# The prologue and the first mixer of a two-layer trunk written as one planned task list, with two DMA queues

## The chip, the cores and the metric

The program runs on one core of a Trainium2 chip as one launch. The metric is the device time of that launch in microseconds. The kernel before takes 1396.52 us, the median of 3 runs (1395.69 to 1398.09).

## The reference

The trunk has 512 tokens of width 1024 and two layers, all in float32. Layer 0 mixes tokens by windowed attention and by a depthwise convolution of 31 taps side by side, layer 1 by a scanned state space, and a gated feed-forward net follows each. Every norm is scaled, shifted and gated by vectors that are products of `silu(c)` with `w_mod`. Cut to the part around the change:

```python
silu_c = jax.nn.silu(c)
mod = (silu_c @ w_mod[i] + b_mod[i])[:, None, :]
sh_m, sc_m, g_m, sh_f, sc_f, g_f = jnp.split(mod, 6, axis=-1)
h = rmsnorm(x, norm_mix[i]) * (1.0 + sc_m) + sh_m
...
proj = h @ w_in + b_in
q, k, v, conf_in = jnp.split(proj, [ATTN_WIDTH, ATTN_WIDTH + KV_WIDTH,
                                    ATTN_WIDTH + 2 * KV_WIDTH], axis=-1)
attn = swa_sink_attention(q, k, v, sinks, positions)
conf = conformer_conv(conf_in, conv_w, conv_b, ln_g, ln_b)
return jnp.concatenate([attn, conf], axis=-1) @ w_out
...
a, g = jnp.split(u, 2, axis=-1)
h = causal_dwconv(a * jax.nn.sigmoid(g), conv_w, conv_b)
```

## The kernel before, in words

Activations lie with their 1024 features in 8 tiles of 128 partitions, and 512 tokens in the free dimension. A float32 product is made of three matmuls: each factor is cut into a head (`wh`, `hn` with h; ACT writes it, L299) and a rest (`wl`; DVE writes it, L304), and `mm3` (L351 to L353) adds head times head, head times rest and rest times head. Weights come as a stream of 128x1024 tiles (`raw`, 512 KB, L291) into 3 buffers; so a load waits for the rest of an earlier tile, and a product for the head and the rest of its own.

The stages are a prologue, mixer 0, a boundary in halves of 256 columns, the feed-forward net, and the same again for layer 1. Only the prologue and mixer 0 concern us.

**Prologue** (L620 to L760). It squares x for the norm, and for each of 8 steps (`kt`) it loads two 512 KB pieces of `w_mod` (`wss`) and one 384 KB piece of the input projection (`wg`). Two `mod_dot`s on DVE (L569) give the scale and the shift of the step, L695 and L700 write the normed tile's product and rest, ACT its head, and `begin` (L704) issues 18 matmuls into six PSUM banks `g0`, which hold the value and gate halves of convolution channels 0 to 2. The last step's 18 go through `mm3`. The rest of each `wg` tile is made on POOL (`split(g0r[kt], wh, wl, nc.gpsimd)`, L278). POOL also makes the rotary angles: some 35 small instructions (L1132 to L1188), then eight that spread them (L1205); ACT takes their sines (L747), and PE and ACT turn them into tables. Everything here is in the order in which it is written, with loads three steps ahead.

**Mixer 0.** Its work is a list of tasks with an engine, a cost and predecessors each. `Plan.run` (L129) simulates them with these costs and emits each engine's instructions in the order in which the simulation starts them; the table `MIXER0` adds a weight to each label and group. The tasks are: eight products of weight tiles (the value and gate of convolution channel 3, k, v, four q); for each of four channel groups a sigmoid, a product on DVE (`gated`), a store of the result to DRAM (`conv_store`, L792), four loads that read it back shifted (`conv_fetch`, L804, tile `s`, 270 KB each), a load of the taps as block-diagonal matrices (`conv_taps`, L797, 512 KB each) and 64 matmuls (`conv_product`, L811); four attention heads of scores, maxima, exponentials (L921), turns (L941), values, reciprocals spread over rows (L973); the norm of the convolution; and the output products. Beside that, 24 pieces of `w_mod` are loaded (L561) and dotted (L569); the boundary needs the first eight.

The shifted loads read overlapping windows, four taps by 32 channels by 540 tokens:

```python
nc.sync.dma_start(u4[g], bass.AP(src.tensor, src.offset + 32 * g * CROW,
                                 [[1, CTAPS], [CROW, 32], [1, CWIN]]))
```

All these DMAs are issued by SP. SP, like every engine, runs in order: a DMA that has to wait for a buffer holds what is behind it. The n-th DMA of SP also waits for the (n-8)-th to land, since eight semaphores count them.

Of the kernel before, what the change touches and what calls it, by code (L numbers as in the profile page):

```python
# [39 lines left out]
_VEC = [("bmod", 96), ("nmix", 16), ("nffn", 16), ("fnorm", 8), ("bin", 14), ("ccw", 124),  # L40
# [30 lines left out]
EARLY = 2  # L71
# [6 lines left out]
MIXER0 = {'sigmoid': -134, 'square': 32, 'osq_add': 34, 'head': -75, 'tap0': -113, 'attn_h': 106, 'conv_h': 47, 'out_c': 124, 'gated': 56, 'rest': 35, 'values': 23, 'rope': -136, 'rstd': 138, 'mod_sum': 7, 'attn_l': 28, 'var': -26, 'turn': 5, 'mod_end': 106, 'exp': -35, 'bring': -32, 'conv_sum': 54, 'out_a': -99, 'osq': -119, 'mod_act': -104, 'mod_add': 39, 'mod_free': 120, 'normalize': -150, 'load': -55, 'product': 71, 'mean_row': -71, 'mod_dve': 105, 'tap': -30, 'recip': 55, 'ln': 121, 'centre': 30, 'residual': -18, 'maxima': 26, 'rstd_row': 20, 'conv_l': 108, 'mean': 47, 'rope_in': 141, 'v_bias': 101, 'mod_load': 69, 'mod_dot': -97, 'root': -10, 'rows': -58, 'rows_in': 61, 'v_turn': 7, 'v_in': -3, 'mod 2': 18, 'head 0': 104, 'mu': -68, 'keys': 27, 'conv 0': 16, 'head 1': -47, 'mod 1': -115, 'head 3': -150, 'shifts': -127, 'scores': 66, 'mod 0': 94, 'conv 3': -77, 'conv 2': 93, 'cbias': -51, 'conv': -113, 'store': -126, 'taps': -47, 'conv 1': 18, 'head 2': 150}  # L78
# [14 lines left out]
class Task:  # L93
    def __init__(self, ways, after, take, give, bonus):
        self.ways, self.after, self.take, self.give, self.bonus = ways, after, take, give, bonus
        self.next = []
# [10 lines left out]
class Plan:  # L107
# [4 lines left out]
    ENGINES = ("PE", "ACT", "DVE", "POOL", "DMA", "SIDE")  # L112

# [4 lines left out]
    def add(self, label, eng, cost, fn, after=(), take=None, give=None, bonus=0.0, table=None):  # L118
        return self.either(label, [Way(eng, cost, fn, table=table)], after, take, give, bonus)

    def either(self, label, ways, after=(), take=None, give=None, bonus=0.0):
        t = Task(ways, [a for a in after if a is not None], take or {}, give or {}, bonus)
        t.label, t.group = label, self.group
        for a in t.after:
            a.next.append(t)
        self.tasks.append(t)
        return t

    def run(self, weight, dry=False):  # L129
        room = dict(self.room)  # L130
        height, wait, at = {}, {}, {}
        for n, t in reversed(list(enumerate(self.tasks))):
            height[t] = min(w.cost for w in t.ways) + max([height[n] + self.LATENCY for n in t.next], default=0.0)
            wait[t], at[t] = len(t.after), 0.0
# [7 lines left out]
        for t in self.tasks:  # L142
            if not t.after:
                release(t)
        free = dict.fromkeys(self.ENGINES, 0.0)
        free.update(self.busy)
        left, now, ends = len(self.tasks), 0.0, []
        gone, table = set(), None
        while left:
            again = True  # L150
            while again:
                again = False
                for e in self.ENGINES:
# [23 lines left out]
                    free[e] = now + w.cost + cold  # L177
                    if w.table not in (None, table):
                        free[e] += self.TABLE
                        table = w.table  # L180
# [29 lines left out]
def trunk(ctx: ExitStack, tc: tile.TileContext, xT_d, vecs_d, rows_d, dsk_d, pos_d, const_d, wss_d, wg0_d,  # L210
          w_d, wmod_d, wdt_d, wcv_d, out_d):
# [68 lines left out]
    class Stream:  # L280
# [47 lines left out]
        def plan(self, plan, count, bonus, more, pool=True):  # L328


            out, last, prev = [], None, None
            for i in range(self.taken, self.taken + count + more):
                n = _STREAM[i] / 8
                t = None
                if i >= len(self.hl):
                    if i >= len(self.raw):
                        last = t = plan.add("load", "DMA", 1.46 * n, lambda i=i: self.load(i + 1), [last], dict(raw=1))
# [206 lines left out]
    def condition(cp):  # L544

        cb = cp.tile([P, KT * P], F32, name="cb")
        mod_pool.append(cb)
        c_ = con[:, 2 * P:]
        act(c_, c_, AF.Silu)
        for i in range(2):  # L550
            ps = spread(c_[:, 4 * i:4 * i + 4])
            yield
            nc.vector.tensor_copy(cb[:, i * T:(i + 1) * T], ps)
            yield

# [3 lines left out]
    def mod_load(n):  # L559
        t_ = mod_raw()  # L560
        nc.sync.dma_start(t_, wmod_d[n])  # L561
        return t_
# [35 lines left out]
    def plan_mods(plan, lo, hi, early):  # L598

        ends, dots, loaded = [], [], None  # L600
        for n in range(lo, hi):
            st, plan.group = {}, f"mod {n // 8}"

            def load(st=st, n=n):
                st["r"] = mod_load(n)

            if n < len(early):
                st["r"] = early[n]
            else:
                loaded = plan.add("mod_load", "DMA", 1.46, load, [loaded], dict(mr=1))  # L610
            dots.append(plan.add("mod_dot", "DVE", 1.22, lambda st=st, n=n: mod_dot(st["r"], mod_at(n)),
                                 [loaded], None, dict(mr=1)))
            if n % 8 == 7:
                ends.append(plan.add("mod_end", "DVE", 0.15, lambda n=n: mod_end(MOD_ORDER[n // 8]), dots))
                dots = []
# [6 lines left out]
    def even_layer(lp, cp, dp0):  # L622
# [5 lines left out]
        def load_first(j):  # L628
            ssr.append([])
            for i in range(2):  # L630
                t_ = mod_raw()
                nc.sync.dma_start(t_, wss_d[j, i])
                ssr[j].append(t_)
            t_ = wp.tile([P, NG0, P], F32, tag="raw", name=nm("raw"), bufs=3)
            nc.sync.dma_start(t_, wg0_d[j])
            g0r.append(t_)

# [3 lines left out]
        for kt in range(KT):  # L641
            nc.sync.dma_start(x[:, kt, :], xT_d[:, kt, :])
        nc.sync.dma_start(vecs, vecs_d)
        ssr, g0r, hn = [], [], []
        for j in range(3):
            load_first(j)
        cond = condition(cp)
        step(cond)

        acc = new_ssq()  # L650
        act(acc, x[:, 0, :], AF.Square)
        late = None
        for k in range(1, KT):
            sq = tmp()
            act(sq, x[:, k, :], AF.Square)
            if k < KT - 1:
                tt(acc, acc, sq, ALU.add)
            else:
                late = sq
            if k in (3, 4):  # L660
                step(cond, 2)
        for i, wch in enumerate((1, 4, 7, 10)):
            ts(b1[:, i, :], bm[:, wch, :], 1.0, None, ALU.add)
        gain = small(8)
        tt(gain, b1[:, 0, :], vec("nmix", 0, 8), ALU.mult)
        act(small(1), eps[:, 0:1], AF.Sqrt)
        g0 = [bank() for _ in range(NG0)]

# [5 lines left out]
        warm(WARM[0])  # L674
        total = token_sums([late, acc])
        warm(WARM[1])
        angles = []
        angle = rope_angles(lp, tile_s, angles)
        rope_t = {}
        tables = rope_tables(angles, tile_s, rope_t)  # L680
        step(angle, 14)

        def scale(kt):
            G = modv[:, 1, kt:kt + 1]
            mod_dot(ssr[kt][0], G)
            act(G, G, AF.Identity, bias=gain[:, kt:kt + 1], scale=vec("nmix", kt))

        def shift(kt):
            S = modv[:, 0, kt:kt + 1]
            mod_dot(ssr[kt][1], S)  # L690
            act(S, S, AF.Identity, bias=bm[:, 0, kt:kt + 1])

        def scaled(kt):
            t = tmp()
            stt(t, x[:, kt, :], modv[:, 1, kt:kt + 1], rb, ALU.mult, ALU.mult)  # L695
            return t

        def lower(kt, t):
            h, l = hn[kt]
            stt(l, t, modv[:, 0, kt:kt + 1], h.bitcast(F32), ALU.add, ALU.subtract)  # L700

        def begin(kt, w, a):
            for i in range(NG0):
                mm(g0[i], lhsT=w[:, i, :], rhs=a, start=(kt == 0 and w is wh and a is hn[0][0]), stop=False)  # L704

        wh = t = early = None
        for kt in range(KT):
            scale(kt)
            if kt == 0:
                col0 = rstd_cols(total, 1024.0)  # L710
                rb = spread(col0)
                warm(WARM[2])
                shift(kt)
            else:
                lower(kt - 1, t)
            t = scaled(kt)
            if kt > 0:
                begin(kt - 1, wh, hn[kt - 1][1])
            wh = wp.tile([P, NG0, P], F32R, tag="wh", name=nm("wh"))
            wl = wp.tile([P, NG0, P], F32R, tag="wl", name=nm("wl"))  # L720
            split(g0r[kt], wh, wl, nc.gpsimd)
            if kt > 0:
                shift(kt)
            h, l = hn_tile("h"), hn_tile("l")
            act(h, t, AF.Identity, bias=modv[:, 0, kt:kt + 1])
            hn.append((h, l))
            if kt < KT - 1:
                begin(kt, wh, h)
                begin(kt, wl, h)
            step(angle, 8)  # L730
            if kt + 3 < KT:
                load_first(kt + 3)
            elif kt + 3 == KT:
                W.load(3)
                nc.sync.dma_start(rows, rows_d.broadcast_to([P, NROW]))
                mk = tile_s((P, 2 * P))
                nc.sync.dma_start(mk, const_d[:, 2 * P + 8:])
                for i in range(2):
# [1096 lines left out]
```

## Time and profile before

| | |
|---|---|
| median of 3 runs | 1396.52 us (1395.69 to 1398.09) |
| the profiled execution | 1396.99 us, span 1395.2 us |
| PE busy | 1335.4 us, 96% of the span |
| DVE busy | 877.5 us, 63% |
| ACT busy | 555.6 us, 40% |
| POOL busy | 95.6 us, 7% |
| chain that ended last | PE 81%, DMA 7%, DVE 5%, issue 2%, ACT 2%, POOL 2% |

The span is the stretch that the profiler sees, the execution's own time has 1.8 us around it. "Busy" is summed over instructions, so a busy engine may be slow as well. The chain follows the last instruction back, at each step to what released it.

### The profile page before, as it was taken

How to read it: one execution, taken by the hardware profiler on the slowest of the kernel's cores; microseconds unless marked ns; L12 is line 12 of the kernel's file. 1: busy time of each engine (PE TensorE's matmuls, PEld its weight loads, DVE VectorE, ACT ScalarE, POOL GpSimd, SP SyncE). 2: the span in 40 equal slices, each digit the busy share in tenths (PEclk: the TensorE clock that was granted, in tenths of full speed). 3: DMA queues.
4: the chain of work that ended last, by engine and by line, in shares of the span. 5: the costliest groups of instructions: out<-in, count | busy, mean ns of one | idle time of the engine just before them, and what ended most of it. 6: DMA issues, size and time to landing. Idle time of an engine off the chain costs nothing.

```text
span 1395.2 us, 17487 instructions
## 1 busy us (share of the span) xinstructions
PE 1335.4 (96%) x6829; PEld 1090.8 (78%) x6831; DVE 877.5 (63%) x1435; ACT 555.6 (40%) x811; POOL 95.6 (7%) x132
## 2 busy tenths in 40 slices
PE   6958989999999999999997999999999999999997
PEld 5746448988888888888885788887898888888886
DVE  7746545777566666667787785888776434434533
ACT  5414434443223223336554363555354313322333
POOL 7600000000000000010010100100000000000001
PEclk8988999999999999999998999999999999999998
DMA  8685531366465575432532332432323333323221
GB/s 307 210 253 176 182 105 61 107 185 219 151 216 173 171 232 176 137 104 65 150 114 96 120 110 83 149 93 84 109 61 121 91 93 103 97 86 111 95 66 61
DMA packets 57699, 185.75 MB, mean 133 GB/s; under 512 B 7824, under 2 KB 10896, under 8 KB 57616
## 3 DMA queue, kind: packets, MB, share of 16 engines
q1 hardware_dynamic: 53056, 172.44, 38.9%
q0 software_dynamic: 3872, 11.54, 2.6%
q8 instruction: 53, 0.87, 0.3%
q10 hardware_dynamic: 688, 0.66, 0.1%
q14 instruction: 30, 0.25, 0.1%
HBM read 181.34 MB, written 3.28 MB: 132 GB/s over the span
## 4 chain that ended last, share of the span: by engine, by line
PE 81%; DMA 7%; DVE 5%; issue 2%; ACT 2%; POOL 2%; SPq 0%; DVEq 0%; POOLq 0%; ACTq 0%
PE ps L351 25%; PE ps L352 25%; PE ps L353 25%; DMA mr<-in_wmod_dram 3%; DMA raw<-in_w_dram 2%; DVE mr L569 1%; PE ps L704 1%; PE ps L1517 1%; PE ps L377 1%; DMA M<-scr 1%; PE ps L1509 1%; PE ps L385 1%; PE ps L1495 1%; POOL wl L278 1%; DVE wl L304 1%
## 5 line engine op out<-in xcount | busy, mean ns | idle before, releaser
L351 PE MATMUL ps<-hn,wh 128*128 128x512 f32 (+1 forms) x1214 | 462.0, 381 | 13.5 <-ACT wh L299 12.7
L353 PE MATMUL ps<-hn,wl 128*128 128x512 f32 (+1 forms) x1214 | 456.1, 376 | 1.2 <-DVE wl L304 1.2
L352 PE MATMUL ps<-hn,wh 128*128 128x512 f32 (+1 forms) x1214 | 456.2, 376 | 0.4
L299 ACT CAST wh<-raw 128x1024 fp32r<-128x1024 f32 (+1 forms) x208 | 212.8, 1028 | 281.3 <-PE ps L352 233.1
L304 DVE TENSOR_TENSOR wl<-raw,wh 128x1024 fp32r<-128x1024 f32 (+1 forms) x208 | 250.7, 1209 | 95.0 <-ACT wh L299 93.7
L351 PEld LDWEIGHTS ps<-hn,wh 128*128 128x128 f32 x1214 | 230.1, 190 | 56.6 <-ACT wh L299 13.9
L353 PEld LDWEIGHTS ps<-hn,wl 128*128 128x128 f32 x1214 | 229.8, 189 | 43.7 <-DVE wl L304 2.4
L352 PEld LDWEIGHTS ps<-hn,wh 128*128 128x128 f32 x1214 | 230.2, 190 | 42.2 <-issue 1.2
L440 DVE SCALAR_TENSOR_TENSOR x<-ps,modv,x 128x512 f32<-128x512 f32 (+1 forms) x108 | 74.3, 690 | 132.9 <-PE ps L353 132.9
L569 DVE SCALAR_TENSOR_TENSOR mr<-mr,cb 128x1024 f32<-128x1024 f32 x96 | 120.8, 1267 | 39.4 <-DMA mr<-in_wmod_dram 39.4
L351 PE MATMUL ps<-fh,wh 128*128 128x512 f32 (+1 forms) x380 | 142.2, 374 | 0.0
L352 PE MATMUL ps<-fl,wh 128*128 128x512 f32 (+1 forms) x380 | 141.9, 373 | 0.0
L353 PE MATMUL ps<-fh,wl 128*128 128x512 f32 (+1 forms) x380 | 141.9, 373 | 0.0
L1226 DVE SCALAR_TENSOR_TENSOR tmp<-ps,vecs,tmp 128x511 f32<-128x511 f32 x44 | 32.9, 748 | 79.9 <-ACT tmp L1225 79.9
L352 PEld LDWEIGHTS ps<-fl,wh 128*128 128x128 f32 x380 | 71.5, 188 | 12.7
L351 PEld LDWEIGHTS ps<-fh,wh 128*128 128x128 f32 x380 | 71.5, 188 | 12.7
L353 PEld LDWEIGHTS ps<-fh,wl 128*128 128x128 f32 x380 | 71.5, 188 | 12.6
L1225 ACT ACTIVATE tmp<-ps,vecs 128x512 f32<-128x512 f32 x44 | 34.3, 779 | 115.4 <-PE ps L353 115.4
L415 POOL TENSOR_TENSOR ssq<-ssq,tmp 128x512 f32<-128x512 f32 x10 | 13.3, 1332 | 773.2 <-ACT tmp L414 773.2
L277 ACT CAST fh<-tmp 128x512 fp32r<-128x512 f32 x44 | 27.3, 620 | 96.4 <-DVE tmp L1230 96.4
L1228 ACT ACTIVATE tmp<-tmp 128x512 f32<-128x512 f32 x44 | 27.8, 633 | 74.9 <-DVE tmp L1227 74.9
L278 DVE TENSOR_TENSOR fl<-tmp,fh 128x512 fp32r<-128x512 f32 x44 | 30.5, 693 | 30.2 <-ACT fh L277 30.2
(270 smaller groups left out, 1466.6 us busy)
## 6 DMA issues: line engine op xcount, KB each, us to landing
raw<-in_w_dram SPq DMA_DIRECT2D x176, 512.0 KB
mr<-in_wmod_dram SPq DMA_DIRECT2D x80, 512.0 KB
raw<-in_w_dram SPq DMA_DIRECT2D x32, 448.0 KB
mr<-in_wss_dram SPq DMA_DIRECT2D x16, 512.0 KB
M<-scr POOLq DMA_DIRECT2D x16, 512.0 KB, 4.4
s<-uc SPq DMA_DIRECT2D x16, 270.0 KB
raw<-in_wg_dram SPq DMA_DIRECT2D x8, 384.0 KB
E<-scr POOLq DMA_DIRECT2D x32, 96.0 KB, 2.8
```

The source lines that it names most:

```text
L277: nc.scalar.copy(h, src)
L278: (eng or nc.vector).tensor_tensor(l, src, h.bitcast(F32), ALU.subtract)
L299: nc.scalar.copy(h, self.raw[i].rearrange("p (k m) -> p k m", m=P))
L304: eng.tensor_tensor(l, self.raw[i].rearrange("p (k m) -> p k m", m=P), h.bitcast(F32), ALU.subtract)
L351: mm(ps, lhsT=w[0], rhs=ah, start=first, stop=False)
L352: mm(ps, lhsT=w[0], rhs=al, start=False, stop=False)
L353: mm(ps, lhsT=w[1], rhs=ah, start=False, stop=last)
L440: stt(x[:, m, hs], ps, gate(m), x[:, m, hs], ALU.mult, ALU.add)
L569: stt(raw, raw, 1.0, mod_pool[2], ALU.mult, ALU.mult, accum_out=out)
L1225: act(c, pg, AF.Identity, bias=vec("fcb", i), scale=vec("fcw", 3 * i + 2))
L1226: stt(c[:, 1:], pg[:, :T - 1], vec("fcw", 3 * i + 1), c[:, 1:], ALU.mult, ALU.add)
L1228: act(c, c, AF.Silu)
```

## The change

The prologue becomes tasks of the same plan (groups "norm", "first 0" to "first 7", "side"), ahead of mixer 0's, so the planner may interleave their instructions. `EARLY`, the hand-set lead, goes, and all weights of `MIXER0` are new. In the plan a second queue, SIDE, stands beside DMA; with `shared` both draw on one modelled pipe, and `follow` keeps loads in order without waiting for the earlier one's end. On the chip SIDE is POOL's queue: the stores, the shifted loads, the 24 pieces of `w_mod` and the margins of the stored rows are issued by POOL. The block-diagonal taps are no longer loaded (4 loads of 512 KB): DVE builds each by one product of a unit matrix and the taps. The rests of the eight `wg` tiles move from POOL to DVE. Seven additions of squares on DVE become 32 matmuls with one column each (`x_sum`); three additions at the boundary move from POOL to DVE. POOL's angle instructions are written up front, and the spreading, turning and copying of the tables are tasks. What follows mixer 0 is unchanged on every engine.

```diff
+        if self.shared and e in ("DMA", "SIDE"):
+            free[e] = pipe = max(now, pipe) + w.cost
...
-                    split(g0r[kt], wh, wl, nc.gpsimd)
+        def wg_rest(kt):
+            h, l = st["w", kt]
+            tt(l, st["wg", kt], h.bitcast(F32), ALU.subtract)
...
-        t_ = mod_raw()
-        nc.sync.dma_start(t_, wmod_d[n])
+        (queue or nc.sync).dma_start(t_, wmod_d[n])
...
+            loaded = plan.add("mod_load", "SIDE", 1.5, load, (), dict(mr=1), follow=loaded)
...
         def conv_store(i):
-            nc.sync.dma_start(rows_c[i][:, CPAD:CPAD + T], us[i])
+            nc.gpsimd.dma_start(rows_c[i][:, CPAD:CPAD + T], us[i])
...
-            st["cw", i] = mod_raw().rearrange("p (g q c) -> p g q c", g=4, q=CQ)
-            nc.sync.dma_start(st["cw", i], wcv_d[i])
+            t_ = mod_raw().rearrange("p (n c) -> p n c", c=32)
+            tt(t_, vec("eye", 0, 32).unsqueeze(1).broadcast_to([P, 32, 32]),
+               vec("ccw", 32 * i, 32).unsqueeze(2).broadcast_to([P, 32, 32]), ALU.mult)
...
-                nc.sync.dma_start(u4[g], bass.AP(src.tensor, src.offset + 32 * g * CROW,
+                nc.gpsimd.dma_start(u4[g], bass.AP(src.tensor, src.offset + 32 * g * CROW,
...
+        t = add("angles", "POOL", 38.0, nothing)
+        t = add("sines", "ACT", 0.5, lambda: [act(a_, a_, AF.Sin) for a_ in angles], [t], table="sin")
...
+            c_ = plan.add("store", "SIDE", 1.0, lambda: conv_store(i), [b_])
+            c_ = plan.add("shifts", "SIDE", 3.6, lambda: conv_fetch(i), [c_, margins_], dict(u4=1))
...
-                plan.add("osq_add", "POOL", 1.2, lambda m=m: pool.tensor_tensor(acc, acc, st["osq", m], ALU.add),
+                plan.add("osq_add", "DVE", 0.69, lambda m=m: tt(acc, acc, st["osq", m], ALU.add),
```

Three places show how the order moves. The first is SP's queue where mixer 0 begins: `raw` is the weight stream, `mr` a piece of `w_mod` or taps, `s` a shifted load, `uc` a stored channel group. Before:

```order
L291 DMA raw_723<-in_w_dram 128x1024
L561 DMA mr_727<-in_wmod_dram 128x1024
L797 DMA mr_730<-in_wcv_dram 128x1024
L804 DMA s_761<-uc_110 128x1x540
L804 DMA s_762<-uc_110 128x1x540
L804 DMA s_763<-uc_110 128x1x540
L804 DMA s_764<-uc_110 128x1x540
L561 DMA mr_781<-in_wmod_dram 128x1024
L291 DMA raw_783<-in_w_dram 128x1024
L792 DMA uc_109<-s_686 128x512
L561 DMA mr_819<-in_wmod_dram 128x1024
L291 DMA raw_824<-in_w_dram 128x1024
```

And with the change, from the last `wg` load on:

```order
L720 DMA raw_525<-in_wg_dram 128x768
L800 DMA s_545<-in_const_dram 128x256
L304 DMA raw_579<-in_w_dram 128x1024
L304 DMA raw_600<-in_w_dram 128x1024
L304 DMA raw_609<-in_w_dram 128x1024
L304 DMA raw_643<-in_w_dram 128x1024
L304 DMA raw_655<-in_w_dram 128x1024
L304 DMA raw_741<-in_w_dram 128x1024
```

The weight loads now follow one another, with no piece of `w_mod` between them.

The second place is POOL's queue after the angles. Before, its rests of `wg` lie among the angle instructions:

```order
L1163 TENSOR_TENSOR s_214<-s_214 128x64
L1150 CAST s_215<-s_214 128x64
L278 TENSOR_TENSOR wl_257<-raw_128,wh_256 128x768
L1152 CAST s_216<-s_215 128x64
L1154 TENSOR_TENSOR s_214<-s_214,s_216 128x64
L1163 TENSOR_TENSOR s_214<-s_214 128x64
L1150 CAST s_215<-s_214 128x64
```

With the change no rest is left there, and after the margins the queue holds these (three stores, the shifted loads of two groups, the last store, and so on to the `w_mod` pieces):

```order
L872 DMA uc_108<-s_653 128x512
L872 DMA uc_109<-s_684 128x512
L872 DMA uc_110<-s_690 128x512
L886 DMA s_704<-uc_108 128x1x540
L886 DMA s_705<-uc_108 128x1x540
L886 DMA s_706<-uc_108 128x1x540
L886 DMA s_707<-uc_108 128x1x540
L886 DMA s_743<-uc_109 128x1x540
L886 DMA s_744<-uc_109 128x1x540
L886 DMA s_745<-uc_109 128x1x540
L886 DMA s_746<-uc_109 128x1x540
L872 DMA uc_111<-s_792 128x512
```

The store of group 3 (`uc_111`) stands ahead of the shifted loads of group 2 (`uc_110`).

The third is DVE early in the prologue, where L569 (L571 after) is a dot, L695 (L741) and L700 (L749) write the normed tile. Before:

```order
L569 SCALAR_TENSOR_TENSOR mr_126,modv<-mr_126,cb 128x1024
L695 SCALAR_TENSOR_TENSOR tmp_254<-x,modv,ps_244 128x512
L569 SCALAR_TENSOR_TENSOR mr_130,modv<-mr_130,cb 128x1024
L700 SCALAR_TENSOR_TENSOR hn_261<-tmp_254,modv,hn_260 128x512
L695 SCALAR_TENSOR_TENSOR tmp_292<-x,modv,ps_244 128x512
L569 SCALAR_TENSOR_TENSOR mr_132,modv<-mr_132,cb 128x1024
L569 SCALAR_TENSOR_TENSOR mr_136,modv<-mr_136,cb 128x1024
L700 SCALAR_TENSOR_TENSOR hn_307<-tmp_292,modv,hn_306 128x512
```

With the change:

```order
L571 SCALAR_TENSOR_TENSOR mr_257,modv<-mr_257,cb 128x1024
L571 SCALAR_TENSOR_TENSOR mr_255,modv<-mr_255,cb 128x1024
L741 SCALAR_TENSOR_TENSOR tmp_314<-x,modv,ps_299 128x512
L729 TENSOR_TENSOR wl_308<-raw_279,wh_307 128x768
L571 SCALAR_TENSOR_TENSOR mr_287,modv<-mr_287,cb 128x1024
L571 SCALAR_TENSOR_TENSOR mr_285,modv<-mr_285,cb 128x1024
L749 SCALAR_TENSOR_TENSOR hn_323<-tmp_314,modv,hn_322 128x512
L741 SCALAR_TENSOR_TENSOR tmp_351<-x,modv,ps_299 128x512
L571 SCALAR_TENSOR_TENSOR mr_318,modv<-mr_318,cb 128x1024
```

The rest of a `wg` tile (L729) has come in among the dots, and a dot pair runs ahead of the normed tile.

## Rows read from the trace of the kernel before

**Rows 1.** Busy time by stretch: us, PE, PEld, DVE, ACT, POOL, PEclk, DMA share, GB/s.
```profile
104.00:122.00 18.00, 17.64 (x76) 12.78 (x77) 12.02 (x25) 8.87 (x24) 0.00 (x0) 0.85 0.67 189
...
129.00:196.00 67.00, 65.59 (x523) 34.05 (x524) 36.23 (x74) 24.75 (x64) 0.00 (x0) 0.97 0.57 175
...
160.00:168.00 8.00, 8.00 (x74) 2.71 (x77) 1.89 (x5) 0.56 (x1) 0.00 (x0) 1.00 0.29 105
...
198.50:212.00 13.50, 11.54 (x92) 9.10 (x92) 8.02 (x19) 9.91 (x26) 0.00 (x0) 0.75 0.00 1
...
212.00:245.00 33.00, 33.00 (x142) 26.92 (x142) 19.21 (x28) 14.25 (x20) 4.14 (x3) 0.95 0.21 64
```

**Rows 2.** Groups of PE instructions, 61.5 to 220 us: busy, mean ns | idle before.
```profile
L351 PE MATMUL ps<-hn,wh 128*128 128x512 f32 x70 | 29.3, 418 | 12.7 <-ACT wh L299 12.7
...
L811 PE MATMUL ps<-s,mr 128*32 128x512 f32 x256 | 29.1, 594 | 0.8 <-DMA s<-uc 0.8
...
L941 PE MATMUL ps<-con,s 128*128 128x128 f32 x56 | 9.7, 315 | 4.6 <-ACT s L921 4.6
...
L973 PE MATMUL ps<-con,sm 128*64 128x128 f32 x64 | 5.4, 317 | 6.1 <-ACT tmp L841 6.1
```

**Rows 3.** Timeline of PE: start, us, engine, line, work [wait before].
```profile
19.83 2.17 PE L704 MATMUL ps<-hn,wh 128*128 128x512 f32 x6
...
61.64 0.39 PE L351 MATMUL ps<-hn,wh 128*128 128x512 f32 x1
...
74.57 0.39 PE L351 MATMUL ps<-hn,wh 128*128 128x512 f32 x1
...
104.32 0.80 PE L351 MATMUL ps<-hn,wh 128*128 128x512 f32 x1 [12.53 <-ACT wh L299]
...
143.66 7.07 PE L811 MATMUL ps<-s,mr 128*32 128x512 f32 x64
...
247.70 0.28 PE L351 MATMUL ps<-s,wh 128*128 128x256 f32 x1
```

**Rows 4.** Waits, 60 to 210 us: who for whom: total us, times, longest.
```profile
ACT wh L299 <- DMA raw<-in_w_dram: 40.4, 5, 18.4
```

**Rows 5.** Waits of SP's queue, 55 to 210 us, in the same columns.
```profile
SPq L561 <- DVE mr L569: 29.9, 8, 11.2
...
SPq L291 <- DMA raw<-in_w_dram: 9.4, 1, 9.4
```

**Rows 6.** Timeline of DVE, in the prologue.
```profile
12.89 1.21 DVE L569 SCALAR_TENSOR_TENSOR mr<-mr,cb 128x1024 f32<-128x1024 f32 x1
...
21.46 0.73 DVE L695 SCALAR_TENSOR_TENSOR tmp<-x,modv,ps 128x512 f32<-128x512 f32 x1
...
22.12 1.21 DVE L569 SCALAR_TENSOR_TENSOR mr<-mr,cb 128x1024 f32<-128x1024 f32 x1
...
23.27 1.24 DVE L569 SCALAR_TENSOR_TENSOR mr<-mr,cb 128x1024 f32<-128x1024 f32 x1
...
36.98 2.27 DVE L700 SCALAR_TENSOR_TENSOR hn<-tmp,modv,hn 128x512 fp32r<-128x512 f32 x1
...
56.81 0.75 DVE L695 SCALAR_TENSOR_TENSOR tmp<-x,modv,ps 128x512 f32<-128x512 f32 x1 [3.46 <-ACT modv L686]
```

**Rows 7.** A group of DVE instructions, 0 to 220 us, by form.
```profile
L304 DVE TENSOR_TENSOR wl<-raw,wh 128x1024 fp32r<-128x1024 f32 x13 | 15.7, 1220 | 11.7 <-ACT wh L299 11.7
```

**Rows 8.** Timeline of POOL, in the prologue.
```profile
19.73 1.24 POOL L1152 CAST s<-s 128x64 f32<-128x64 int32 x1
...
27.06 2.78 POOL L278 TENSOR_TENSOR wl<-raw,wh 128x768 fp32r<-128x768 f32 x1
...
41.48 0.22 POOL L1188 TENSOR_SCALAR ang<-ang 128x32 f32<-128x32 f32 x1
```

**Rows 9.** DMAs of tile M on POOL's queue: issue ns (min/median/max), window; landing.
```profile
L1455 POOL DMA_DIRECT2D M<-scr x16: 577/580/649, 684.8 to 953.6; - x16
...
DMA to landing us min/median/max: 4.1/4.4/7.9
```

More of the change, by code (lines that the diff above doesn't have):

```diff
@@ L70 @@
 WARM = (2, 2, 3)
-EARLY = 2
 NEXT = 2
@@ L142, in run @@
         for t in self.tasks:
-            if not t.after:
+            if not wait[t]:
                 release(t)
         free = dict.fromkeys(self.ENGINES, 0.0)
+        pipe = 0.0
         free.update(self.busy)
@@ L596, in mod_steps, with plan_mods @@
             yield
-    def plan_mods(plan, lo, hi, early):
-        ends, dots, loaded = [], [], None
+    def plan_mods(plan, lo, hi, after, ready):
+        ends, dots, loaded = [], [], after
         for n in range(lo, hi):
@@ L640, in even_layer @@
         nc.gpsimd.memset(zeros, 0.0)
[L641 to L666, printed above, removed]
-        g0 = [bank() for _ in range(NG0)]
+        cb = cp.tile([P, KT * P], F32, name="cb")
+        mod_pool.append(cb)
+        cond = con[:, 2 * P:]
+        act(cond, cond, AF.Silu)
+        angles, rope_t, turned = [], {}, []
+        for _ in rope_angles(lp, tile_s, angles):
+            pass
+        wide = []
+        for which in range(2):
+            wide.append(tile_s((P, NCH, P)))
+            nc.gpsimd.memset(wide[which], 1.0 - which)
+        g0 = [bank() for _ in range(NG0)]
+        hn = [None] * KT
+        st = {}
+        plan = Plan(dict(ACT=4.6, DMA=2.2, PE=4.9, DVE=1.2), ps=8 - NG0, tmp=6, mr=6, u4=2, units=UNITS, **W.room())
+        plan.shared = True
+        add = plan.add
         def warm(n):
@@ L672, in warm @@
                 mm(g0[NG0 - 1][:, 0:2 * P], lhsT=ident, rhs=con[:, :2 * P], start=True, stop=True)
[L674 to L681, printed above, removed]
+        plan.group = "norm"
+        xs_, last = [], None
+        for k in range(KT):
+            last = add("x_load", "DMA", 0.75, lambda k=k: nc.sync.dma_start(x[:, k, :], xT_d[:, k, :]), follow=last)
+            xs_.append(last)
@@ L768, in even_layer @@
         po = [None] * 4
-        plan = Plan(dict(PE=2.3, DVE=1.8, POOL=0.5, DMA=2.5), ps=8 - NG0, tmp=6, mr=6 - len(early), u4=2, units=UNITS, **W.room())
-        tiles = W.plan(plan, 16, 3.0, NEXT, False)
+        plan.group = ""
+        tiles = W.plan(plan, 16, 3.0, NEXT, False, last, prev)
         def pe_product(n, name):
@@ L1086, in even_layer @@
         gate = mcol(2)
-        ends = plan_mods(plan, 0, MODS_FIRST, early)
+        ends = plan_mods(plan, 0, MODS_FIRST, last, [mask_, *cbs])
         acc = new_ssq()
```

311 lines of the change are left out of this document (172 added, 139 removed).

## The prediction, on record before the changed kernel was run

> **What bounds the kernel now.** The page's first part shows PE busy for 96% of the span, so only stretches where PE waits or runs slowly can give time back. What follows mixer 0 is the same work in the same order in both programs, so I look at the first 250 us alone. The timeline of PE gives its ends: the last prologue step's first matmul starts at 61.64 us and the first 256-column matmul of the boundary at 247.70 us [rows 3], 186.06 us apart. Whatever shortens the way to 61.64, and whatever those 186.06 us lose, is what the change can win.
>
> In the 186.06 us, read the idle time at the end of each row of PE's groups [rows 2]: 12.7 us before the products' first matmuls, 6.1 before the spread reciprocals, 4.6 before the turns behind an exponential, 0.8 before the convolutions, together 24.2. Then read the clock beside PE's busy time [rows 1]: 17.64 us at 0.85, 65.59 at 0.97, 11.54 at 0.75 and 33.00 at 0.95, so (1 - clock) times busy time is 2.6 + 2.0 + 2.9 + 1.65 = 9.2 us. The granted clock has two levels, 2.4 and 1.2 GHz, and these means lie between; the low ones stand in the stretches after PE has waited. So 33.4 of the 186.06 us are lost and 152.7 are work.
>
> Who causes the loss? The one long hole ends at 104.32, after 12.53 us, on a weight head of ACT [rows 3]; ACT in turn waited five times, 40.4 us in all and 18.4 once, for the DMA that brings the tile [rows 4]. And the weight loads were late because SP, which issues everything, stood still: 29.9 us at loads of `w_mod` that waited for a buffer to be dotted and 9.4 at a weight load that waited for an earlier one to land [rows 5]. The 6.1 us hole hangs on the same in-order ACT. So the early mixer is bound by one queue's order, not by an engine.
>
> The prologue is bound otherwise. Its timeline of DVE shows dots 1.15 us apart (22.12 to 23.27) and a 128x512 step of 0.66 (21.46 to 22.12), but also one that took 2.27 at 36.98 [rows 6], while POOL ran a rest of 2.78 us [rows 8]: the two stretch each other. At 56.81 DVE had waited 3.46 us for ACT [rows 6].
>
> **The change, part by part.** *Prologue.* DVE's work from its first dot, at 12.89 [rows 6]: 16 dots x 1.15 = 18.4; 8 rests of 128x768, three quarters of the 1.22 us of a 128x1024 one [rows 7], so 0.92 each and 7.3; 16 steps x 0.66 = 10.6. That is 36.3 and ends at 49.2. PE, from 19.83 [rows 3]: 57 matmuls took 74.57 - 61.64 = 12.93 us, 0.227 each, so the 126 before the last step need 28.6 and end at 48.4. POOL's angle chain: from 19.73 to 41.70 it did 24 small instructions and two rests, (21.97 - 5.55) / 24 = 0.68 us each [rows 8]; without the rests it ends near 36.2. ACT reaches the sines at about 31.5 by DVE's count (ten dots, three rests, six steps), so it stands for some 5 us; PE has 24 matmuls, 5.4 us, to bridge that. I add 3.8 us for waits between the engines and take **53** for the start of the last step. Bounds: 49.2, and 61.6 if nothing is won. Gain 61.64 - 53 = 8.6. The seven additions removed from DVE, the 32 one-column matmuls and the `vecs` rows that are 36 numbers longer lie before 12.89, beside the loads of x: nothing.
>
> *Weight stream.* SP now issues weights alone, each waiting only for a rest. The pipe can keep up: in 104 to 122 us it gave 189 GB/s at a share of 0.67 [rows 1], and a product of 24 matmuls (5.45 us) uses 0.52 MB, 96 GB/s. So the holes of 12.7 and 6.1 go, and most of the half clock behind them. What is late next is DVE, which has to make the rests, all 24 dots and 4 taps (0.92 to 1.22 us each by [rows 7], 4 to 5 us in all, paid beside PE's products) in the same stretch.
>
> *Convolutions.* They move ahead of the heads: after the last step PE does the two products of channel 3 (48 x 0.227 = 10.9 us) and then all four convolutions of 7.07 us [rows 3]. The first needs its shifted loads at 53 + 4.1 + 10.9 = 68. First gated at 55.8, stored by POOL and landed at about 58.5, then four loads: an issue is 0.58 us and a 512 KB landing 4.4 [rows 9], so about 58.5 + 4 x 0.58 + 4.4 = 65.2: hidden. That is POOL's price. The same loads on SP are bounded by 160 to 168, where the pipe carried little beside shifted loads: share 0.29, 105 GB/s [rows 1], so 1.1 MB takes 10.5 us. Between 4.4 and 10.5 I take POOL's row, as the queue that now issues. The Trainium skill, "DMA: Bandwidth & Descriptors", section "Why a DMA increments its semaphore by 16 and not by 1", says that a transfer is spread over as many engines, up to 16, as divide the outermost size on both sides, and that SP's queue takes the lowest-numbered while POOL's turns through them. The outermost size here is 4, and the row's 0.29 agrees with four of sixteen; no run here shows the second half. By it a group would take some 2.7 us, an estimate from that page; my sum does not change by it.
>
> *The other moves.* POOL's three additions at the boundary go to DVE, with PE busy for all of 212 to 245 [rows 1]: nothing. The 2 MB of taps that are not read any more free the pipe where weights were late, which is in the weight term.
>
> *What is left over.* The exponentials' 4.6 stay. For new waits I take 3 (0 if the plan's order holds, 6.1 as the second hole was), and 3.5 for half clock after them (0 to 9.2): 11 us instead of 33.4, a gain of 22.4.
>
> *Sum.* 53 + 152.7 + 11 = 216.7 for the boundary instead of 247.70, 31.0 less. The profiled execution took 1396.99, so 1366.0; it lies 0.47 above the median, so **1365.5** as a median.
>
> **The rivals.**
> - *The shifted loads stay slow on POOL's queue too* (10.5 us a group, one after another). Groups would land at 58.5 + 10.5 = 69, 79.5, 90 and 100.5, and PE, which has the four in a row, would wait 1 + 3 x 3.4 = 11.2; at half clock after each, of which 104 to 122 us cost 2.6 [rows 1], some 8 more: 19 us, 1384.5. For it: the share of 0.29 [rows 1]. Against: PE waited 0.8 for convolutions before [rows 2], though they stood later.
> - *The second queue brings nothing:* weights stay late, because the pipe, not the issue, sets them, and only the prologue's 8.6 are won: 1388. Against: the 29.9 us for dots [rows 5]. The Trainium skill, same page, section "Issuing engines are not separate DMA queues", speaks for it: queues share the engines, and a second issuer saves only issue time. In this trace the loss is a queue held by a wait, which that sentence doesn't cover.
> - *The sines hold the prologue.* POOL's instructions at 1.24 each [rows 8], 24 of them from 19.73, end at 49.5. ACT stands before the sines, three steps of 18 matmuls hang behind it (another 12 us), and nothing is won ahead of 61.6: 1374.
> - *POOL's queue goes one DMA at a time; slower.* If each has to land before the next, at 4.4 us [rows 9], the last group of shifts, 20 DMAs after 57, lands at 145 instead of before 89. PE's order has the fourth convolution ahead of the heads, so the mixer ends 56 us later: 1421. It decides from 3.15 us a DMA on, where 57 + 20 x 3.15 = 120 eats the 31 won. Against: issues of 0.58 us [rows 9], 16 of them without a note of such waiting.
> - *It does not come out:* the framework's own placing or new waits eat the gain, within 0.2%.
>
> **How the numbers follow.** Forecast 0.54, slow shifts 0.19, no gain from the queue 0.07, sines 0.07, serial POOL 0.08, nothing 0.05. A measurement of this kernel can tell some 0.2% from no change, 2.8 us. Faster is the first four, 0.87; the same 0.05; slower 0.08. The range: at its low end the prologue ends at 49.2 and half of the exponentials' wait goes with all other loss, 49.2 + 152.7 + 2.3 = 204.2, 43.5 less: 1353. At its high end it takes in sines and most of the slow shifts: 1387. The last rivals, 0.13 and some edge, stay out.
>
> **What would show it.** Right: no long wait of SP for a dot, PE's holes before products gone, last prologue step near 53, convolutions one after another from 68, the 256-column matmuls from about 217. Slow shifts: waits of PE for `s` before L893, at a share near 0.29. Sines: ACT idle before L823 by 10 us. Serial POOL: the issues several us apart. It would be wrong above all if DVE, given the rests, dots, taps and the heads' maxima at once, becomes what PE waits for: then rests and maxima are late and the left-over 11 grows.

## The result, and the profile after

| | before | changed |
|---|---|---|
| median | 1396.11 us (1394.26 to 1398.09, 4 runs) | 1375.86 us (1374.55 to 1377.46, 4 runs) |
| ratio, 95% interval | | 0.9855 [0.9837, 0.9873] |
| the profiled execution, span | 1396.99, 1395.2 us | 1374.55, 1372.8 us |
| last prologue step starts | 61.64 us [rows 3] | 57.01 us |
| first 256-column matmul | 247.70 us [rows 3] | 225.52 us |

It is 20.3 us faster; 31 were forecast. The two landmarks in PE's timeline of the changed kernel say where: 4.6 us are won before the last prologue step, 17.5 between it and the boundary, none after.

```profile
25.76 1.66 PE L753 MATMUL ps<-hn,wh 128*128 128x512 f32 x6
...
57.01 0.39 PE L365 MATMUL ps<-hn,wh 128*128 128x512 f32 x1
...
74.26 1.04 PE L893 MATMUL ps<-s,mr 128*32 128x512 f32 x2 [1.15 <-DMA s<-uc]
...
78.77 1.92 PE L893 MATMUL ps<-s,mr 128*32 128x512 f32 x2 [3.46 <-DMA s<-uc]
...
82.63 8.97 PE L893 MATMUL ps<-s,mr 128*32 128x512 f32 x64 [1.94 <-DMA s<-uc]
...
94.12 14.62 PE L893 MATMUL ps<-s,mr 128*32 128x512 f32 x122 [2.53 <-DMA s<-uc]
...
225.52 0.28 PE L365 MATMUL ps<-s,wh 128*128 128x256 f32 x1
```

The first row is the prologue's first matmul, which was at 19.83 [rows 3]: the prologue starts 5.9 us later, and ends earlier. The four L893 rows are waits inside the first two convolutions, in which PE stood for shifted loads. PE's groups from 57 to 231 us (busy, mean ns | idle before) count the loss:

```profile
L893 PE MATMUL ps<-s,mr 128*32 128x512 f32 x256 | 34.7, 630 | 9.1 <-DMA s<-uc 9.1
L365 PE MATMUL ps<-hn,wh 128*128 128x512 f32 x70 | 28.8, 412 | 0.0
...
L1023 PE MATMUL ps<-con,s 128*128 128x128 f32 x56 | 8.2, 280 | 1.9 <-ACT s L1003 1.6
...
L1055 PE MATMUL ps<-con,sm 128*64 128x128 f32 x64 | 4.8, 282 | 1.2 <-DVE sm L1010 1.2
```

The holes of 12.7 before the products (L351, now L365) and 6.1 before L973 (now L1055) [rows 2] have become 0 and 1.2; that of the convolutions grew from 0.8 to 9.1. By stretch (columns as in [rows 1]):

```profile
57.00:72.00 15.00, 15.00 (x67) 12.20 (x65) 10.72 (x11) 7.12 (x8) 7.08 (x11) 1.00 0.69 207
...
72.00:94.00 22.00, 13.04 (x71) 2.71 (x70) 4.33 (x4) 3.46 (x4) 3.32 (x5) 0.77 1.06 215
...
94.00:109.00 15.00, 14.88 (x123) 5.59 (x124) 0.00 (x0) 0.85 (x2) 4.91 (x8) 1.00 0.94 204
```

Around the two waiting convolutions the granted clock was 0.77, which costs 0.23 x 13.04 = 3.0 us, and the DMA engines were busy throughout (1.06) while moving only 215 GB/s. The issues of 50 to 130 us (KB each, median us to landing) and two pieces of the chain that ended last show where to look:

```profile
raw<-in_w_dram SPq DMA_DIRECT2D x11, 512.0 KB, 5.1
...
s<-uc POOLq DMA_DIRECT2D x16, 270.0 KB, 15.3
```

```profile
9.16 11.29 PE ps L679 x64
...
73.94 21.30 DMA uc<-s
```

A shifted load of 270 KB took 15.3 us, a weight load of 512 KB 5.1, and one store 21.3 behind the shifted loads of POOL's queue. In the prologue the one-column matmuls of the norm (L679) hold the chain for 11.3 us.

### The profile page after: what moved, and what is told of

Its sections match the earlier page's. It is cut to its first block, busy times and chain, and to the rows that moved or that the text cites. A ratio compares the mean times of both kernels' runs of the same rounds, so it can differ in the third digit from the quotient of the medians.

```text
span 1372.8 us, 17568 instructions
## 1 busy us (share of the span) xinstructions
PE 1334.5 (97%) x6878; PEld 1092.3 (80%) x6879; DVE 876.2 (64%) x1444; ACT 555.5 (40%) x811; POOL 95.7 (7%) x173
## 2 busy tenths in 40 slices
DMA packets 58212, 183.71 MB, mean 134 GB/s; under 512 B 10064, under 2 KB 13200, under 8 KB 58128
## 4 chain that ended last, share of the span: by engine, by line
PE 83%; issue 8%; DMA 4%; DVE 3%; ACT 1%; POOL 1%; DVEq 0%; POOLq 0%; ACTq 0%
PE ps L365 25%; PE ps L367 25%; PE ps L366 25%; DMA uc<-s 2%; PE ps L753 1%; PE ps L399 1%; PE ps L1573 1%; PE ps L391 1%; DMA M<-scr 1%; PE ps L679 1%; DVE mr L571 1%; PE ps L1565 1%; DMA s<-uc 1%; PE ps L1551 1%; POOL mr L563 0%
## 5 line engine op out<-in xcount | busy, mean ns | idle before, releaser
L365 PE MATMUL ps<-hn,wh 128*128 128x512 f32 (+1 forms) x1214 | 461.3, 380 | 0.8 <-ACT hn L441 0.8
L365 PEld LDWEIGHTS ps<-hn,wh 128*128 128x128 f32 x1214 | 229.2, 189 | 43.5 <-issue 1.7
L365 PE MATMUL ps<-fh,wh 128*128 128x512 f32 (+1 forms) x380 | 142.2, 374 | 0.0
L571 DVE SCALAR_TENSOR_TENSOR mr<-mr,cb 128x1024 f32<-128x1024 f32 x96 | 116.1, 1218 | 4.6 <-DMA mr<-in_wmod_dram 2.5
L366 PEld LDWEIGHTS ps<-fl,wh 128*128 128x128 f32 x380 | 71.5, 188 | 12.7
L367 PEld LDWEIGHTS ps<-fh,wl 128*128 128x128 f32 x380 | 71.5, 188 | 12.7
L365 PEld LDWEIGHTS ps<-fh,wh 128*128 128x128 f32 x380 | 71.5, 188 | 12.6
## 6 DMA issues: line engine op xcount, KB each, us to landing
s<-uc POOLq DMA_DIRECT2D x16, 270.0 KB, 15.3
```

The lines of the kernel that those rows point to most:

```text
L365: mm(ps, lhsT=w[0], rhs=ah, start=first, stop=False)
L366: mm(ps, lhsT=w[0], rhs=al, start=False, stop=False)
L367: mm(ps, lhsT=w[1], rhs=ah, start=False, stop=last)
L571: stt(raw, raw, 1.0, mod_pool[2], ALU.mult, ALU.mult, accum_out=out)
```

## The experiments

"The changed kernel" and "the kernel before" are the two bases; each run changes only what its diff shows, and the runs of one group share their runs of the kernel before (medians 1395.8, 1395.7 and 1394.9 us for the three groups, 1395.6 for the last run). Where a run has no interval it is one execution.

### First group: undo or do one part

**The norm's sums on DVE**, in the changed kernel:

```diff
-            st["xq", k] = tmp()
+            st["xq", k] = tmp() if k else new_ssq()
...
-            for c in range(NCH):
-                mm(st["xt"][:, c:c + 1], lhsT=st["xq", k][:, c * P:(c + 1) * P], rhs=ones,
-                   start=(k == 0 and c == 0), stop=(k == KT - 1 and c == NCH - 1))
+            elif k < KT - 1:
+                tt(st["xq", 0], st["xq", 0], st["xq", k], ALU.add)
+            else:
+                for j in (k, 0):
...
```

> The changed kernel with the squares of x added on DVE again (six additions) and two groups of one-column matmuls instead of eight; all else in the same order. Theory A, that the 64 one-column passes hold PE and the norm (11.3 us on the chain from 9.2 to 20.5 us): the first matmul of the first step comes near 20 instead of 25.8 us, the last step starts at 51 to 52.5 instead of 57.0, and the time falls by 4 to 6 us against 1375.9, to about 1371. Theory B, that DVE's own count sets the prologue (36 us of work from its first dot): the start comes earlier but the last step moves by less than 2 us, and the time stays within 2 us.

1373.67 us (1372.63 to 1379.12), ratio 0.9839 [0.9823, 0.9856], 2.2 below the changed kernel with intervals that overlap. PE's timeline, in the profiled execution (which was the slowest of the four, 1379.12):

```profile
22.74 1.73 PE L756 MATMUL ps<-hn,wh 128*128 128x512 f32 x6
...
54.08 0.39 PE L365 MATMUL ps<-hn,wh 128*128 128x512 f32 x1
...
81.94 9.69 PE L896 MATMUL ps<-s,mr 128*32 128x512 f32 x64 [3.62 <-DMA s<-uc]
```

Start and last step come 3.0 and 2.9 us earlier, half of what A expected. But the first convolution's last wait ends at 81.94 against 82.63, and PE's wait for shifted loads grew from 9.1 to 12.5: the loads, asked for 2.9 us sooner, arrived at nearly the same time. In this execution, what the prologue won was lost again at the DMA; the other three took 1372.6 to 1373.8 us and have no trace.

**The shifted loads on SP**, in the changed kernel:

```diff
-                nc.gpsimd.dma_start(u4[g], bass.AP(src.tensor, src.offset + 32 * g * CROW,
+                nc.sync.dma_start(u4[g], bass.AP(src.tensor, src.offset + 32 * g * CROW,
```

> The changed kernel with the 16 shifted loads issued by SP again, in the plan's order between the weight loads; the stores and the pieces of w_mod stay on POOL. Theory A, one pipe that the shifted loads and the weights share: PE's wait for the first convolutions stays at 9 us, within 3, and the time within 3 us of 1375.9. Theory B, POOL's queue is the slow part (13 to 17 us a load against 10.5 us for a group on SP): the wait falls to 4 us or less and the time by 5 or more. Theory C, a queue in order: the weight loads behind the shifts wait for the stores, holes come before the products, and the time rises by 5 to 15 us.

1398.08 us: slower by 22 and back at the time of before. PE's wait for shifted loads, and the worst stretch:

```profile
L893 PE MATMUL ps<-s,mr 128*32 128x512 f32 x256 | 42.3, 686 | 21.5 <-DMA s<-uc 21.5
```

```profile
72.00:94.00 22.00, 13.02 (x69) 2.65 (x68) 3.11 (x3) 1.73 (x2) 2.15 (x4) 0.77 0.63 193
```

None of the three theories: the rise is more than C's 5 to 15 us, and it is not at C's holes but at the convolutions, where the wait is 21.5 us. Here the DMA engines are busy by 0.63 only, and the loads are late all the same.

**The pieces of `w_mod` on SP**, in the changed kernel:

```diff
-                st["r"] = mod_load(n, nc.gpsimd)
+                st["r"] = mod_load(n)
```

> The changed kernel with the 24 pieces of w_mod issued by SP again, as the plan orders them between the weights. Theory A, weights were late because SP stood at loads of w_mod that wait for a dot: holes before products come back, 8 to 18 us in all, and the time is 1384 to 1394. Theory B, the plan's order did it, with eight weight loads ahead of the first piece: no hole over 2 us and the time within 3 us of 1375.9.

1384.31 us, at the low end of A, but again in another place: no hole before a product, and the wait for shifted loads 13.5 instead of 9.1.

**The pieces of `w_mod` on POOL**, in the kernel before (the 20 that its plan loads):

```diff
-                st["r"] = mod_load(n)
+                st["r"] = mod_load(n, nc.gpsimd)
```

> The kernel before with one part of the change alone: the 20 pieces of w_mod that the plan loads are issued by POOL, and every other instruction keeps its order. Theory A, the held queue was the loss in mixer 0: the 12.7 us hole before the products and the 6.1 us hole go, with some 4 us of half clock, and the time falls by 15 to 22 us, to 1374 to 1381. Theory B, the pipe itself was late (2 MB of taps, 12 MB of w_mod, the shifts): the holes stay within 4 us of what they were, and the time falls by less than 5.

1391.41 us, ratio 0.997 [0.996, 0.998]: a gain of 4.4, where theory A, on which the prediction stood, asked for 15 to 22. The time is theory B's, though its holes are not: the one before the products shrank to 2.5, the one before L973 stayed at 6.2, and one of 4.8 opened before the scores. SP's waits for a dot were not all gone, since the taps use the same buffers:

```profile
SPq L797 <- DVE mr L569: 8.3, 2, 5.3
```

That is 8.3 us instead of 29.9 [rows 5]. Between 60 and 140 us the chain runs through these pieces (start, us, what):

```profile
88.00 19.89 DMA uc<-s
...
110.22 16.72 DMA raw<-in_w_dram
```

With no `w_mod` issued by SP in that stretch, a store took 19.9 us and a weight load 16.7. Both were issued right behind four shifted loads. This points away from SP's wait for a dot, to something that the shifted loads do to what follows them.

### Second group: what the shifted loads do

**The shifted loads on POOL**, in the kernel before:

```diff
-                nc.sync.dma_start(u4[g], bass.AP(src.tensor, src.offset + 32 * g * CROW,
+                nc.gpsimd.dma_start(u4[g], bass.AP(src.tensor, src.offset + 32 * g * CROW,
```

> The kernel before with another part of the change alone: the 16 shifted loads are issued by POOL; stores, taps, pieces of w_mod and weights stay on SP in their order. Theory D, new after the first four runs: a shifted load runs on few of the 16 DMA engines, and what follows it on SP's queue, the weights too, lands only when those engines are through (a landing of some 12 us behind it). Then this run takes the 12.7 and 6.1 us holes away where moving w_mod did not: a gain of 12 to 20 us, 1376 to 1384. Theory A, SP stands at the loads of w_mod that wait for dots: the holes stay, gain under 5 us.

1379.7 us, ratio 0.989 [0.9874, 0.9906]: a gain of 16.0 us, against the change's 20.3, from this one line, although SP still waited 34.9 us for dots. The holes shrank to 5.1 and 4.1. The loads themselves are not fast there, and the weights are slow beside them:

```profile
raw<-in_w_dram SPq DMA_DIRECT2D x12, 512.0 KB, 10.6
...
s<-uc POOLq DMA_DIRECT2D x11, 270.0 KB, 15.1
```

**The rows turned**, in the kernel before. A shifted load writes 128 partitions, and its source is four taps of 32 channels; now channels are outside:

```diff
-                                                       [[1, CTAPS], [CROW, 32], [1, CWIN]]))
+                                                       [[CROW, 32], [1, CTAPS], [1, CWIN]]))
...
-    r["wcv"] = diag.reshape(4, P, 4, CQ, 32)
+    r["wcv"] = diag.transpose(0, 2, 1, 3, 4, 5).reshape(4, P, 4, CQ, 32)
```

> The kernel before with the rows of the shifted loads turned in the same way and the loaded taps packed to match; nothing else, no instruction moves, one queue. Theory D: the 12.7 and 6.1 us holes and most of the half clock behind them go, a gain of 12 to 22 us, without a second queue and without a new order. Theory A or P (dots, or the amount of data): a gain under 4 us.

1366.64 us (1365.56 to 1368.77), ratio 0.9793 [0.9779, 0.9808]: 29 us, more than the whole change and more than theory D's 12 to 22, with one queue and the old order. A stretch, the landing of a shifted load, and the boundary:

```profile
72.00:94.00 22.00, 16.82 (x75) 12.15 (x74) 17.83 (x29) 6.73 (x8) 0.00 (x0) 1.00 0.98 357
```

```profile
s<-uc SPq DMA_DIRECT2D x12, 270.0 KB, 5.2
```

```profile
218.07 0.28 PE L351 MATMUL ps<-s,wh 128*128 128x256 f32 x1
```

The pipe moves 357 GB/s at a share of 0.98. In the kernel before, the stretch at 0.29 and 105 GB/s [rows 1] belongs to a group of shifted loads that SP issued between 147.64 and 150.20 us, with four pieces of `w_mod` right behind them. The same time in pieces of 2 us:

```profile
150.00:152.00 2.00, 2.00 (x22) 1.17 (x16) 1.28 (x3) 1.20 (x3) 0.00 (x0) 1.00 0.26 95
...
156.00:158.00 2.00, 2.00 (x10) 1.68 (x9) 0.00 (x0) 0.00 (x0) 0.00 (x0) 1.00 1.03 244
...
164.00:166.00 2.00, 2.00 (x24) 0.65 (x20) 0.00 (x0) 0.00 (x0) 0.00 (x0) 1.00 0.25 104
```

At first, when little but the shifted loads moves, 0.26 of 16 engines are busy, which is 4.2 of them, and the outermost size of the source was 4. Then the pieces of `w_mod` keep all engines busy, and at the end a quarter of them is still at work. The packets of SP's queue over the whole execution, before and with the rows turned, fit this:

```profile
q1 hardware_dynamic: 53056, 172.44, 38.9%
...
q1 hardware_dynamic: 53248, 172.44, 38.9%
```

The bytes are the same and the packets 192 more, 12 for each of the 16 loads, which is 16 less 4. (In the changed kernel, with the loads on SP, the counts are 47296 and 47488, again 192 apart.) The Trainium skill, "DMA: Bandwidth & Descriptors", section "Why a DMA increments its semaphore by 16 and not by 1", gives the rule for the number of engines (the largest number up to 16 that divides the outermost sizes of both sides); 4 before and 16 after agree with the rows. No view names the engines of a transfer, so what follows is inferred from shares and counts: an unturned load on SP fills the queues of about four engines, and a transfer behind it that uses all is complete only when those four are through. This would account for the 16.7 us.

**The rows turned**, in the changed kernel, on POOL and on SP (unit matrix and taps packed to match; the second with the diff of the run on SP above):

```diff
-                                                       [[1, CTAPS], [CROW, 32], [1, CWIN]]))
+                                                       [[CROW, 32], [1, CTAPS], [1, CWIN]]))
...
-        "eye": np.tile(np.eye(32, dtype=np.float32), (CTAPS, 1)),
+        "eye": np.repeat(np.eye(32, dtype=np.float32), CTAPS, axis=0),
```

> The changed kernel with the order of the rows inside a shifted load turned, channel outside and tap inside (32, 4 instead of 4, 32), and the unit matrix and the taps packed to match; the same bytes, the same instructions, still on POOL's queue. Theory P, the pipe is full at 70 to 95 us whatever the spread: PE's wait for the first two convolutions stays 9 to 12 us and the time within 3 us of 1375.9. Theory D for POOL's queue too: each load was confined to few DMA engines; the wait falls to 4 us or less and the time by 5 to 12 us.

> The same turned rows, with the shifted loads on SP's queue (the run with unturned rows on SP took 1398.1 us). Theory D: the weights behind the shifts are no longer held and the shifts themselves land in 4 to 6 us: 1365 to 1378 us. Theory C, SP's order (weights behind shifts that wait for a store) was what cost 22 us: it stays above 1390.

1364.91 us (1362.53 to 1365.39), ratio 0.9774 [0.9758, 0.979], and 1364.73. On SP the turned rows are worth 33 us, on POOL 11, and then the queue makes no difference. On POOL the first convolutions no longer wait:

```profile
72.00:94.00 22.00, 21.62 (x192) 6.42 (x192) 4.33 (x4) 4.15 (x5) 7.02 (x13) 1.00 0.94 361
```

So POOL's queue was not free of the trouble, only hurt less. There the engines were busy while the loads were late (1.06, above), so four engines at a time do not account for it, and why unturned loads are slow on POOL stays open. The changed kernel with turned rows lies 1.7 us below the kernel before with turned rows, with intervals that overlap: once the shifted loads are spread, the change as it stands can't be told from none by its time. At the boundary it is 5.5 us ahead in the profiled executions (212.58 against 218.07), but it runs on longer at the very end (last section).

### Third group: what is left of the change

**Turned rows and the norm's sums on DVE** (both diffs above, on the changed kernel), and **turned rows with everything on SP's one queue**, the margins too:

```diff
-            nc.gpsimd.dma_start(rows_c[i][:, CPAD:CPAD + T], us[i])
+            nc.sync.dma_start(rows_c[i][:, CPAD:CPAD + T], us[i])
...
-                nc.gpsimd.dma_start(u4[g], bass.AP(src.tensor, src.offset + 32 * g * CROW,
+                nc.sync.dma_start(u4[g], bass.AP(src.tensor, src.offset + 32 * g * CROW,
...
-                st["r"] = mod_load(n, nc.gpsimd)
+                st["r"] = mod_load(n)
```

> The changed kernel with both the turned rows of the shifted loads (1364.9 us alone) and the squares of x added on DVE (1373.7 alone, where the last prologue step started at 54.1 instead of 57.0 us and the convolutions then waited for the pipe). Theory: with the shifts spread the convolutions no longer wait, so the 2.9 us of the earlier start reach the end: 1361 to 1363. Rival: the shifts, asked for 2.9 us earlier, are late again by as much: 1364 to 1366.

> The changed kernel with turned rows and everything back on SP's one queue: stores, shifted loads, margins and the 24 pieces of w_mod. Theory D: once the shifted loads are spread, the second queue has nothing left to give, and the time stays within 4 us of 1364.9. Theory A, a load that waits for a dot holds the weights behind it: holes come back and the time is 1372 or more.

1359.05 us, ratio 0.9741 [0.9726, 0.9755], and 1358.73, ratio 0.9736 [0.9719, 0.9752]. With the loads spread, the gain of the sums does reach the end. The time fell by 5.9 us, more than expected: the last step starts 2.8 us earlier, at 54.21, the boundary comes 5.9 earlier, at 206.65, and where the other 3.1 come from was not asked. And one queue is not slower than two; it is even faster, 0.9736 against 0.9774, by more than the 4 us that theory D allowed. The boundary comes at 210.77 instead of 212.58, and most of the rest of the difference lies at the very end (last section). On this one queue SP waits for dots about as long as in the kernel before, 28.1 us against 29.9 [rows 5]:

```profile
SPq L563 <- DVE mr L571: 28.1, 15, 6.6
```

The time is 36 us below that kernel's, so such waits cost little here, where the shifted loads are spread.

**The rests of `wg` on DVE**, alone, in the kernel before:

```diff
-            split(g0r[kt], wh, wl, nc.gpsimd)
+            split(g0r[kt], wh, wl)
```

> The kernel before with one line of the prologue changed: the rests of the eight wg tiles are made by DVE, in the place where they stand, not by POOL. Theory, DVE and POOL stretch each other: the last prologue step starts at 55 to 59 us instead of 61.6, and the time falls by 2 to 6 us. Rival, DVE has 7 us more to do and is what the prologue waits for: no earlier start, and within 2 us of before or slower.

1389.77 us, ratio 0.9961 [0.9946, 0.9975]: 5.1 us. PE's timeline, and its group with the hole before the products:

```profile
54.12 0.43 PE L351 MATMUL ps<-hn,wh 128*128 128x512 f32 x1
```

```profile
L351 PE MATMUL ps<-hn,wh 128*128 128x512 f32 x70 | 29.5, 421 | 12.2 <-ACT wh L299 12.2
```

The last step starts at 54.1 instead of 61.6. That one line brings 7.5 us in the prologue, more than the whole planned prologue, which brought 4.6 and lost 2.9 to its sums; with the sums back on DVE, the planned one reaches 53.8 (next run), 0.3 more than this line alone. In the prologue DVE's dots took 1232 ns in the mean instead of 1518 and its normed tiles (L700) 751 instead of 1174, so the reading that DVE and POOL stretch each other is borne out.

**All of it on one queue**: planned order, turned rows, sums on DVE, no DMA of mixer 0 on POOL:

> The planned kernel with turned rows, everything on SP's one queue (1358.7 us in the run before) and the squares of x added on DVE. Theory: the prologue's last step starts 2.5 to 3 us earlier, at 54 us, no hole opens behind it, and the time is 1355 to 1357, the fastest here. Rival: on one queue the earlier start meets later weights, and it stays at 1358 to 1360.

1355.25 us (1353.89 to 1356.3), ratio 0.9713 [0.97, 0.9726], the fastest version here, 20 us below the changed kernel. Landmarks, and page part 1:

```profile
53.80 0.39 PE L365 MATMUL ps<-hn,wh 128*128 128x512 f32 x1
...
206.67 0.28 PE L365 MATMUL ps<-s,wh 128*128 128x256 f32 x1
```

```profile
PE 1320.1 (98%) x6830; PEld 1082.9 (80%) x6831; DVE 880.9 (65%) x1450; ACT 555.8 (41%) x811; POOL 74.6 (6%) x121
```

Against the kernel before with turned rows (0.9793) this is 0.8%, about 11 us: that is what order, rests, built taps and the change's smaller moves, without its sums and its second queue, are worth together once the loads are spread.

## Why the prediction was right, and where it was not

The direction and the range (1353 to 1387) held; the gain was two thirds of the 31 us. The boundary came 8.8 us later than the sum's 216.7: 4.0 from the start of the last step, 4.2 from what was left over, 0.6 from the work.

- **Work in the mixer: right.** 152.7 us were taken. Measured: 225.52 - 57.01 = 168.5, less 9.1 + 1.9 + 1.2 idle and 3.0 at half clock, 153.3.
- **Start of the last step: 53 taken, 57.01 measured.** From first matmul to last step PE needed 57.01 - 25.76 = 31.3 us, near the 28.6 of its matmuls with the two tables, and stood for only 0.8 of them, so the sines held nobody. DVE was as full: it worked without a gap from 24.20 to 54.10 us, and the chain runs mostly through it to 36.0 and through PE from 36.8. Both started late, behind the norm, for which DVE stood 4.0 us. The term that failed is "the 32 one-column matmuls ... nothing": they run as 64 instructions of 0.18 us, 11.3 us on the chain, and the start moves from 19.83 to 25.76. With the sums on DVE again 3.0 of these 5.9 us come back; what the other 2.9 are was not tried. (The removed additions are six, not seven; and the rest on POOL that overlaps the 2.27 us step of DVE at 36.98 is one that starts at 35.94 and takes 2.77 us, not the row shown, at 27.06 [rows 8].)
- **Weight stream: right in the holes, wrong in the cause.** The holes of 12.7 and 6.1 went, as summed. But the step "the weight loads were late because SP ... stood still", with the 29.9 us at loads that waited for dots, is refuted as the main cause: moving the planned `w_mod` loads off SP cut these waits to 8.3 and gained 4.4 us, and turning rows gained 29 with all loads of `w_mod` on SP. What is shown is the shifted loads. The trace of the kernel before had it in its chain, where two weight loads, once issued, took 15 us to land:

```profile
88.06 15.09 DMA raw<-in_w_dram
...
111.70 15.43 DMA raw<-in_w_dram
```

  Each stands behind four shifted loads and one piece of `w_mod` in SP's queue. That the holes went all the same was luck: the change took the shifted loads off SP too, for another reason.
- **Convolutions: the term that was mis-sized most.** A landing of 4.4 us was taken from POOL's 512 KB loads [rows 9], "hidden"; measured were 15.3, with 9.1 of wait and 3.0 of half clock. The other bound, 10.5 us a group at a share of 0.29, was the row of the same transfer and nearer. The first shifted load was also issued at 65.21 instead of 58.5. The rival "slow shifts" is what happened, at 12 us instead of 19, since only the first two groups were waited for; its sign, a share near 0.29, did not show, the share was 1.06. The row of 0.29 was in hand, and I read it as a price of the shifted loads, not as a queue that holds everything behind it. It carried more than them: SP had issued four pieces of `w_mod` from 150.28 us on, so the 10.5 us are no price of the group alone.
- **Second queue.** The rival that it brings nothing named the pipe as the reason; the Trainium skill, "DMA: Bandwidth & Descriptors", section "Issuing engines are not separate DMA queues", speaks for it. The runs bear it out for spread loads (one queue 1358.7, two 1364.9). For unspread ones, moving them to the second queue gave 16 us, with the weights no longer behind them on SP.
- **Left over: 11 taken, 15.2 measured**, of which 12.1 are the convolutions; the exponentials' 4.6 fell to 1.9.
- **Serial POOL and the sines** did not occur: shifted loads were issued 0.68 us apart.

The parts don't add: shifted loads 16.0, rests 5.1 and `w_mod` 4.4 alone make 25.5, against 20.3 for the change. It also moved the convolutions ahead of other work that could have covered the slow loads, and put the sums on PE; that this is the difference is not shown.

## What to carry to other kernels

Look at the DMA share while a transfer is late: a share that stands at a fraction (0.25 to 0.29 here) with loads waiting can mean that the transfer runs on few engines, and that everything behind it in that queue waits for them. A full share does not clear it: on POOL it was 1.06, and only the rate (215 GB/s, 361 when turned) gave the loads away. Try an access pattern that has a size with a factor of 16 outermost, before queues or orders are changed. And when the profile names a long wait at an issuing engine, remove that wait alone once: here cutting it from 29.9 to 8.3 us was worth 4.4.

## What the runs showed of the hardware

- The same 4.4 MB of shifted loads land in 15.3 us each on POOL with four taps outside; with 32 channels outside in 6.9 on POOL, and on SP in 5.2, or 7.2 in the run that leaves stores and `w_mod` on POOL (medians). On POOL unturned, the engines were busy (1.06) at 215 GB/s, turned 361 at 0.94. The page counts 10064 packets under 512 B unturned and 6992 turned; whether these 3072 small packets cost the rate was not tried.
- The 32 one-column matmuls, which the profile counts as 64, took 0.18 us each; a 512-column one of the products takes 0.227 [rows 3]. Part of that is the clock: the first 26 took 3.35 us and the last 26 5.68, with the granted clock at 0.50, the lower level, from 12 us to their end.
- Two turned kernels with `w_mod` on POOL run on for 4.9 us after their last data, the changed kernel for 1.8, the kernel before with turned rows and the one-queue kernel for 1.3. The last stretch of the turned kernel on POOL and of the one-queue kernel, in the columns of [rows 1]:

```profile
1358.50:1363.40 4.90, 0.00 (x0) 0.00 (x0) 0.00 (x0) 0.00 (x0) 0.00 (x0) 0.50 0.00 2
```

```profile
1356.00:1357.30 1.30, 0.00 (x0) 0.00 (x0) 0.00 (x0) 0.00 (x0) 0.00 (x0) 0.50 0.00 0
```

  No engine is busy and nothing is moved. It is most of the advantage of one queue in those executions, and its cause stays open.
